# Seven block products for twelve chunks of a down projection, with weight sums formed in DRAM and the residual added there

## The chip, the cores and the metric

The kernel runs on one core of a Trainium2 chip. The time is that of one launch on the device, in microseconds (us); of several runs the median is given. A traced execution also gives its span, from the first to the last recorded instruction. The engines are TensorE (PE, matmuls; PEld its weight loads), VectorE (DVE), ScalarE (ACT), GpSimd (POOL) and SyncE (SP). SP and POOL issue the DMA transfers that this case is about. PSUM holds the sums of matmuls, SBUF the tiles.

## The reference

One layer of a decoder runs on 512 prompt tokens and 8 x 4 sample tokens, in fp32, with shared weights. A convolution mixer and a sparse attention lie beside each other ahead of a feed-forward part with 22 chunks of 128 hidden columns. What matters here is its end:

```python
x = x + g1 * ((ga * y_a + gb * y_b) @ w['w_out'])
h2 = rmsnorm(x, w['norm2']) * (1 + sc2) + sh2
x = x + g2 * ((jax.nn.silu(h2 @ w['w_gate']) * (h2 @ w['w_up'])) @ w['w_down'])
return x, nsa_state, conv_new
```

D_MODEL is 1024 and D_FF 2816. A final RMSNorm gives y. The other outputs are the new caches; one of them, new_win_sample, is the old window cache moved on by four rows, which the kernel copies from DRAM to DRAM.

## The kernel before, in words

All 544 tokens lie along the free axis, channels along the 128 partitions. A product in fp32 is made of three matmuls (`mm3`, L248): high half by high half, high by low, low by high. ACT writes the high half of an operand (a copy into the reduced type), DVE subtracts it to get the low half. Weights come from DRAM as slabs of up to 1 MB (`slab`, L232), issued by SP into three buffers, and are split after they land. The split weights have two buffers of each kind (`wh`, `wl`, `Wh`, `Wl`).

`seven` (L281) makes two output chunks of 128 columns from one slab with seven block products in place of eight. The slab is four blocks a11, a12, a21, a22. Sums of them are needed: y2 = a21 + a22, y1 = y2 + a11, z1 = a11 + a21, z2 = y1 + a12. The tokens are halved too (272 columns each), and of the right-hand side there are the blocks B11, B21, B22 and the sums T1 to T4, formed once in `combine`. A pair is the generator `wpair` (L329): products A (`wA`), B (`wB`) and C (`wC`), 12 matmuls each, then WY by T2 and T1, WZ by T3; W3 by T4 and WZ by B22 are kept in `late` and issued inside the next pair. So a pair is 84 matmuls of 272 columns. Its splits are W0 (a11, a12), WY, WZ and W3 (a22).

The feed-forward loop runs c2 = 1 to 10 (chunks 2 c2 and 2 c2 + 1; chunks 0 and 1 are made earlier). A round is a gate pair, whose outputs go through Silu into `G`, and an up pair, whose outputs are collected in `U` and multiplied into `G`, then split into `f_hilo` (`up_out`, L1717). The down projection has three phases, `PHASES = ((0, 8), (8, 8), (16, 6))`. The first two are plain (`down_part`, L1735), after rounds 3 and 7: for each of 8 output blocks m and each half of the tokens, 8 chunks by three matmuls into `dn`, then `residual` (L1550) on DVE adds the scaled result to `x1`, which stays in SBUF. The last phase is mixed with the final norm.

For c2 = 1 three of the sums are begun by DMA: SP copies a21 from DRAM into SBUF and POOL adds another block to it with an accumulating transfer (L312, L314). The copies of the window cache (`win_shift`) are issued by SP in the rounds c2 = 2 to 9.

The order in which each engine gets its instructions is fixed when the program is built, by a scheduler that goes by the program text and the dependencies. An engine then works through its own list in order: an instruction that waits holds up all behind it.

Of the kernel before, what the change touches and what calls it, by code (L numbers as in the profile page):

```python
# [1941 lines left out]
```

## Time and profile before

| | us |
|---|---|
| runs before | 1228.72, 1228.92, 1230.36 |
| median | 1228.92 |
| profiled execution | 1229.26 |
| its span | 1227.5 |
| feed-forward, first matmul of c2 = 1 to the last phase | 865.46 to 1173.83 |
| last phase and end | 1173.83 to 1227.5 |

How to read the rows: a row of single instructions has its start, its duration, engine, line of the program, operation, the tile written and read, the shape, and in brackets how long the engine stood idle before it and whom it waited for. Matmuls are pipelined, so that the durations of neighbours overlap. A row of a group has count, total busy time and mean duration in ns, then idle time ahead of it and who ended that. A row of windows has the busy time of each engine in a stretch. In DMA rows the last number is the median time from issue to landing.

### The profile page before, as it was taken

The numbers are of one execution on the slowest core, as the hardware profiler recorded it, in microseconds if no ns is written. First come the engines' busy times: TensorE is split into PE (matmuls) and PEld (weight loads), VectorE is DVE, ScalarE is ACT, GpSimd is POOL, SyncE is SP. The second block draws the span as 40 slices with busy tenths as digits, with TensorE's granted clock in tenths as the row PEclk, the third lists the DMA queues.
The fourth block names the chain that finished last, engine by engine and source line by source line (L and its number), as shares of the span: only waits on it lengthen the run. The fifth ranks groups of instructions, "written<-read, shape, count | busy, mean of one in ns | idle before, by whom it ended". The sixth has DMA issues, their size and how long they took to land.

```text
span 1227.5 us, 25476 instructions
## 1 busy us (share of the span) xinstructions
PE 1209.9 (99%) x10230; PEld 1117.1 (91%) x10230; DVE 844.1 (69%) x1868; ACT 631.4 (51%) x1214; POOL 54.8 (4%) x105
## 2 busy tenths in 40 slices
PE   8999999999999999999999999999999999999997
PEld 6998999999999988887777778999999999999996
DVE  4467646897776376676767766758975678666866
ACT  5456545665445333376666675427653255424542
POOL 1000220000000111110000000001000000000000
PEclk9999999999999999999999999999999999999999
DMA  8954234664344997975563325424533423333212
GB/s 282 407 199 155 88 123 149 215 200 164 141 136 145 355 355 277 305 235 163 174 166 121 125 83 213 133 101 138 140 121 121 154 103 137 104 109 132 87 53 73
DMA packets 58920, 205.14 MB, mean 167 GB/s; under 512 B 7208, under 2 KB 13224, under 8 KB 43578
## 3 DMA queue, kind: packets, MB, share of 16 engines
q1 hardware_dynamic: 56898, 199.57, 47.2%
q0 software_dynamic: 1472, 3.56, 1.3%
q8 instruction: 80, 1.31, 0.4%
q10 hardware_dynamic: 432, 0.39, 0.1%
q14 instruction: 38, 0.31, 0.1%
HBM read 181.60 MB, written 29.11 MB: 172 GB/s over the span
## 4 chain that ended last, share of the span: by engine, by line
PE 56%; DVE 1%; ACT 0%; issue 0%; DVEq 0%; ACTq 0%
PE lin L250 5%; PE lin L249 5%; PE lin L251 5%; PE wA L249 4%; PE dn L249 4%; PE dn L251 4%; PE dn L250 3%; PE acc L1440 3%; PE wA L250 3%; PE wA L251 3%; PE ptp L1446 3%; PE wC L251 2%; PE wC L250 2%; PE wC L249 2%; PE modp L401 1%; PE sp L1412 1%
## 5 line engine op out<-in xcount | busy, mean ns | idle before, releaser
L244 ACT ACTIVATE wh<-raw 128x1024 fp32r<-128x1024 f32 x58 | 61.3, 1057 | 99.9 <-PE dn L250 36.8
L249 PE MATMUL lin<-h_h,wh 128*128 128x288 f32 (+1 forms) x352 | 103.8, 295 | 0.0
L250 PE MATMUL lin<-h_l,wh 128*128 128x288 f32 (+1 forms) x352 | 101.6, 289 | 0.0
L251 PE MATMUL lin<-h_h,wl 128*128 128x288 f32 (+1 forms) x352 | 101.2, 288 | 0.0
L245 DVE TENSOR_TENSOR wl<-raw,wh 128x1024 fp32r<-128x1024 f32 x58 | 70.9, 1223 | 26.5 <-ACT wh L244 25.7
L249 PE MATMUL dn<-f_hilo,wh 128*128 128x288 f32 (+1 forms) x304 | 88.0, 291 | 0.1
L251 PE MATMUL dn<-f_hilo,wl 128*128 128x288 f32 (+1 forms) x304 | 87.6, 289 | 0.0
L250 PE MATMUL dn<-f_hilo,wh 128*128 128x288 f32 (+1 forms) x304 | 87.2, 287 | 0.0
L298 ACT ACTIVATE work<-wA 128x272 f32<-128x272 f32 x117 | 46.2, 395 | 66.0 <-PE wA L251 65.0
L1419 ACT ACTIVATE P<-P,nms 128x384 f32<-128x384 f32 (+3 forms) x120 | 65.0, 544 | 20.4 <-DVE nms L1418 19.8
L1418 DVE CUSTOM_DVE_ANT_0 P<-sp,ta 128x384 f32<-128x384 f32 (+3 forms) x120 | 52.4, 470 | 31.5 <-PE sp L1406 24.1
L249 PEld LDWEIGHTS lin<-h_h,wh 128*128 128x128 f32 x352 | 66.8, 190 | 7.7 <-issue 6.2
L650 PE MATMUL phi<-xh,wph 128*128 128x256 f32 x256 | 72.0, 289 | 1.3 <-ACT xh L632 0.7
L650 PE MATMUL phi<-xl,wph 128*128 128x256 f32 x256 | 70.5, 284 | 1.4 <-DVE xl L633 1.4
L383 DVE TENSOR_TENSOR Wl<-ws,Wh 128x1024 fp32r<-128x1024 f32 x39 | 47.8, 1225 | 33.8 <-ACT Wh L382 33.6
L650 PE MATMUL phi<-xh,wpl 128*128 128x256 f32 x256 | 70.2, 283 | 0.0
L250 PEld LDWEIGHTS lin<-h_l,wh 128*128 128x128 f32 x352 | 66.3, 188 | 0.1
L251 PEld LDWEIGHTS lin<-h_h,wl 128*128 128x128 f32 x352 | 66.1, 188 | 0.1
L382 ACT ACTIVATE wh<-raw 128x1024 fp32r<-128x1024 f32 (+2 forms) x43 | 44.4, 1033 | 32.6 <-PE wC L250 13.9
L382 ACT ACTIVATE wh<-ws 128x1024 fp32r<-128x1024 f32 x39 | 41.4, 1062 | 38.3 <-PE wB L250 25.0
L382 ACT ACTIVATE Wh<-ws 128x1024 fp32r<-128x1024 f32 x39 | 41.3, 1059 | 36.4 <-PE wC L250 29.2
L383 DVE TENSOR_TENSOR wl<-ws,wh 128x1024 fp32r<-128x1024 f32 x39 | 47.8, 1225 | 16.1 <-ACT wh L382 15.9
(516 smaller groups left out, 4244.8 us busy)
## 6 DMA issues: line engine op xcount, KB each, us to landing
raw<-in_wt SPq DMA_DIRECT2D x97, 1024.0 KB, 5.3
sraw<-in_cache_sel SPq DMA_DIRECT2D x64, 256.0 KB, 4.7
gt<-in_cache_cmp SPq DMA_DIRECT2D x56, 256.0 KB, 5.5
wraw<-in_cache_winT SPq DMA_DIRECT2D x8, 1024.0 KB, 8.2
out_new_win_sample<-in_cache_win SPq DMA_DIRECT2D x8, 512.0 KB, 5.7
out_new_win_sample<-in_cache_win SPq DMA_DIRECT2D x8, 504.0 KB
raw<-in_wt SPq DMA_DIRECT2D x4, 768.0 KB, 4.2
xT<-in_xT SPq DMA_DIRECT2D x1, 2176.0 KB, 13.5
```

Of the source, the lines that this page charges most:

```text
L244: act.activation(oh, view, AF.Copy)
L245: dve.tensor_sub(ol, view, oh.bitcast(F32))
L249: pe.matmul(p, lhsT=wh[:, k, :], rhs=xh, start=start, stop=False, **kw)
L250: pe.matmul(p, lhsT=wh[:, k, :], rhs=xl, start=False, stop=False, **kw)
L251: pe.matmul(p, lhsT=wl[:, k, :], rhs=xh, start=False, stop=stop, **kw)
L298: o_.snap_ops.append(act.activation(t, p, AF.Copy))
L382: act.activation(hi, src, AF.Copy)
L383: return dve.tensor_sub(lo, src, hi.bitcast(F32))
L650: pe.matmul(po[:, s * 256:s * 256 + 256], lhsT=w, rhs=m, start=(n_ == 0), stop=(n_ == len(ops) - 1))
L1418: p_ops.append(dve.tensor_tensor_reduce(out=t[:, 0:n], in0=sps[br], in1=t_dist[:, 512 - n:512], scale=-hs, scalar=3e38, op0=ALU.add, op1=A ...
L1419: e_ops.append(act.activation(t[:, 0:n], t[:, 0:n], AF.Exp, scale=-1.0, bias=nms[:, c:c + 1], accum_out=sums[:, c:c + 1]))
L1440: pe.matmul(acc[br * 64:br * 64 + 64, :], lhsT=vtok[br][:, j, g * 64:(g + 1) * 64], rhs=pts_[br], start=(j == 0), stop=False)
```

## The change

The phases of the down projection become (0, 4), (4, 6), (10, 6), (16, 6). The first, four chunks, stays plain but moves into round c2 = 2 (`down_plain`); the second and third, six chunks each, are made by `seven` with three chunks on each side of a block (`down_seven`, in rounds 5 and 8): four pairs of 7 x 3 x 3 matmuls each. The last phase is as before. For the seven products the results of the up pairs of rounds 2 to 7 are also needed in sums, which `up_seven` forms on DVE and splits.

The sums y2 and z1 of 28 slabs (20 gate and up slabs, 8 of the down projection) are formed in DRAM long before (`presum`): SP copies a21 twice into a DRAM tile, and one call later POOL adds a22 and a11 to it. The calls lie in the input projection (9), the attention (14) and the output projections. A pair then loads its two sums by one SP transfer of 512 or 384 KB into one of two buffers `ws`, and DVE forms y1 and z2 alone. The order of the blocks inside a slab is changed for that.

The residual x1 is written to DRAM (`x1_dr`, eight SP transfers) when it is formed. Down results are scaled by ACT into staging tiles (`gated`; slices of U and of the G that is not in use) and added in DRAM by 24 accumulating POOL transfers of 272 KB (`add_x1`). Eight SP transfers bring x1 back before the last phase. Its place in SBUF meanwhile holds operands of the new products (`f_x`). Eight of the sixteen window copies move ahead into the output projections.

```diff
-PHASES = ((0, 8), (8, 8), (16, 6))
+PHASES = ((0, 4), (4, 6), (10, 6), (16, 6))
...
+            r6 = np.arange(c0 * 128, (c0 + n) * 128).reshape(n, 128)
+            if ph in (1, 2):
+                quarters(("dn", ph, k2), "w_down", [k2 * 256 + m * 128 + np.arange(128) for m in range(2)], np.concatenate([r6[0::2], r6[1::2]]))
+            else:
+                add(("dn", ph, k2), "w_down", r6, k2 * 256, 256)
...
-        def wslab(*key, summed=0):
+            n_ = len(X[0]) if isinstance(X[0], list) else 4
+            xk = lambda t, k: t[k] if isinstance(t, list) else t[:, k, :]
+            k0 *= n_
+            for k in range(n_):
+                mm3(p, w[0][:, k0:k0 + n_], w[1][:, k0:k0 + n_], xk(X[0], k), xk(X[1], k), k, first and k == 0, k == n_ - 1, skip_group_check=not first)
+
+        def wslab(*key):
             raw = slab(*key)
-            y, z = (wsp.tile([128, 8, 128], F32, tag="ws", bufs=3, name=nm("ws")) for _ in range(2))
-            if summed:
-                src = lambda i: a["wt"][SLAB_AT[key], :, 512 * i:512 * i + 512]
-                for t, i in ((y[:, 4:8], 3), (z[:, 0:4], 0))[0:summed]:
-                    t = t.rearrange("p k f -> p (k f)")
-                    sync.dma_start(t, src(2))
-                    with tc.issue_after(dma_behind.ins):
-                        pool.dma_start(t, src(i), accum_op=ALU.add)
-            return raw.rearrange("p k f -> p (k f)").rearrange("p (n k f) -> p n k f", n=4, k=4), y, z, summed
+            n_ = len(SLABS[key][1]) // 4
+            if key in pre:
+                t = wsp.tile([128, 16, 128], F32, tag="ws", bufs=2, name=nm("ws"))
+                sync.dma_start(t[:, n_:3 * n_].rearrange("p k f -> p (k f)"), pre[key][:, 0:256 * n_])
+                y, z = t[:, 0:2 * n_], t[:, 2 * n_:4 * n_]
+            else:
+                y, z = (wsp.tile([128, 8, 128], F32, tag="ws", bufs=3, name=nm("ws"))[:, 0:2 * n_] for _ in range(2))
+            q = raw.rearrange("p k f -> p (k f)").rearrange("p (n k f) -> p n k f", n=4, k=n_)
+            return q, y, z, key in pre
...
+    x1_dr = [dr.tile([128, NT], F32, name=f"x1_dr{c}") for c in range(8)]
+    pre, pre_keys, copied = {}, [(n, c2) for c2 in range(1, FC // 2) for n in ("fg", "fu")], []
+    for c2 in (8, 5):
+        pre_keys[2 * c2 - 1:2 * c2 - 1] = [("dn", 1 + (c2 == 8), m2) for m2 in range(4)]
+
+    def presum(n=1):
+
+        done = copied[:]
+        del copied[:]
+        for _ in range(min(n, len(pre_keys))):
+            key = pre_keys.pop(0)
+            w_ = len(SLABS[key][1]) // 4 * 128
+            t = pre[key] = dr.tile([128, 1024], F32, name=nm("pre"))
+            src = a["wt"][SLAB_AT[key], :, 0:4 * w_].rearrange("p (n f) -> p n f", n=4)
+            dst = t[:, 0:2 * w_].rearrange("p (n f) -> p n f", n=2)
+            with tc.issue_after(last_slab[0].ins):
+                sync.dma_start(dst, src[:, 1:2].broadcast_to([128, 2, w_]))
+            copied.append((dst, src[:, 0:4:2]))
+        for dst, src in done:
+            pool.dma_start(dst, src, accum_op=ALU.add)
...
+        if hf:
+            sync.dma_start(x1_dr[k], x1[:, k, :])
...
+    f_x = x1_slot("f_x", F32R, WH)[:, 0:14]
+    g2n = modT[:, 0:8, :]
+    act.activation(g2n, g2m, AF.Copy, scale=-1.0)
...
+    def up_seven(G, c2):
+        if c2 % 3 == 2:
+            tt = [f_x[:, 4 * i:4 * i + 4] for i in range(2)]
+            bb = [f_x[:, 8 + i] for i in range(6)]
+        else:
+            tiles = [f6_tile(4 * (c2 % 3 == 0) + i, [128, 4, WH], F32R, "fs") for i in range(4)]
+            tt = tiles[0:2]
+            bb = [tiles[2 + i // 4][:, i % 4] for i in range(6)]
+        ops = fops.setdefault((c2 - 2) // 3, {n: ([], []) for n in ("B11", "B21", "B22", "T1", "T2", "T3", "T4")})
+        for n, i in (("B11", 0), ("B21", 2), ("B22", 4)):
+            for x in range(2):
+                ops[n][x].append(bb[i + x])
+        for n, t, i in (("T1", 0, 0), ("T3", 0, 1), ("T2", 1, 0), ("T4", 1, 1)):
+            for x in range(2):
+                ops[n][x].append(tt[t][:, 2 * x + i])
+        Uf = flat(U)
+
+        def out(m, q, p, s_):
+            if s_ is None:
+                dve.scalar_tensor_tensor(G[:, 1, Q[0]], p, -1.0, G[:, 1, Q[0]], ALU.mult, ALU.mult)
+                to_hilo(G[:, 1, Q[0]], bb[2], bb[3])
+                return
+            dve.tensor_add(U[:, m, Q[q]], p, s_)
+            if m == 1:
+                dve.scalar_tensor_tensor(G[:, 1, Q[1]], U[:, 1, Q[1]], -1.0, G[:, 1, Q[1]], ALU.mult, ALU.mult)
+                to_hilo(G[:, 1, Q[1]], bb[4], bb[5])
+            elif q == 1:
+                dve.tensor_mul(G[:, 0, :], U[:, 0, :], G[:, 0, :])
+                t0, t1, t3 = Uf[:, 0:WH], Uf[:, 2 * WH:3 * WH], Uf[:, 3 * WH:4 * WH]
+                dve.tensor_sub(t0, G[:, 0, Q[0]], G[:, 0, Q[1]])
+                dve.tensor_sub(Uf[:, WH:2 * WH], G[:, 1, Q[1]], G[:, 0, Q[1]])
+                to_hilo(G[:, 0, Q[0]], bb[0], bb[1])
+                pair = lambda i: Uf[:, 2 * i * WH:2 * i * WH + 2 * WH].rearrange("p (k n) -> p k n", k=2)
+                dve.scalar_tensor_tensor(t1, t0, -1.0, G[:, 1, Q[1]], ALU.mult, ALU.subtract)
+                dve.scalar_tensor_tensor(t3, G[:, 1, Q[0]], -1.0, t1, ALU.mult, ALU.subtract)
+                to_hilo(pair(0), tt[0][:, 0:2], tt[0][:, 2:4])
+                to_hilo(pair(1), tt[1][:, 0:2], tt[1][:, 2:4])
+        return out
+
+    def gated(t, c, src, m, g):
+
+        w_ = c.stop - c.start
+        s0 = TS if c.start == 0 else 0
+        act.activation(t[:, c.start + s0:c.stop], src[:, s0:w_], AF.Copy, scale=g[:, m, 0:1])
+        if s0:
+            gbc = g[:, m, 1:9].rearrange("p (b x) -> p b x", x=1).broadcast_to([128, 8, 4])
+            dve.tensor_mul(t[:, 0:TS].rearrange("p (b t) -> p b t", t=4), src[:, 0:TS].rearrange("p (b t) -> p b t", t=4), gbc)
+
+    def add_x1(m, t):
+        pool.dma_start(x1_dr[m], t, accum_op=ALU.add)
+
+    def down_plain():
+
+        nk = PHASES[0][1]
+        stg = [t[:, m, :] for t in (U, Gs[1]) for m in range(2)]
         for m in range(KC):
             if m % 2 == 0:
-                sl_ = slab("dn", ph, m // 2)
+                sl_ = slab("dn", 0, m // 2)
             w = split(sl_[:, :, (m % 2) * 128:(m % 2) * 128 + 128], nk=nk)
+            t = stg[m % 4]
             for hf in range(2):
                 p = lin_ps(nm("dn"))[:, 0:HW[hf]]
                 for k in range(nk):
-                    c = PHASES[ph][0] + k
-                    mm3(p, w[0], w[1], fh[c][:, hcols(hf)], fl[c][:, hcols(hf)], k, k == 0, k == nk - 1)
-                residual(x1, m, hf, p, g2m, f6)
+                    mm3(p, w[0], w[1], fh[k][:, hcols(hf)], fl[k][:, hcols(hf)], k, k == 0, k == nk - 1)
+                gated(t, hcols(hf), p, m, g2m)
+            add_x1(m, t)
+
+    def dn_out(m2, ts):
+        def out(m, q, p, s_):
+            t, g, c = ts[m], (g2m, g2n)[m], Q[q]
+            if s_ is not None:
+                dve.tensor_add(t[:, c], p, s_)
+                p = t[:, c]
+            gated(t, c, p, 2 * m2 + m, g)
+            if m != q:
+                add_x1(2 * m2 + m, t)
+        return out
+
+    def down_seven(ph):
+        o_ = SimpleNamespace(**fops[ph - 1])
+        u0, u1, v0, v1 = (t[:, m, :] for t in (U, Gs[ph - 1]) for m in range(2))
+        for m2, ts in enumerate(((u0, u1), (v0, v1), (u1, u0), (v1, v0))):
+            yield wslab("dn", ph, m2), dn_out(m2, ts), o_
...
     for c2 in range(1, FC // 2):
         G = Gs[c2 % 2]
-        gate = wpair(wslab("fg", c2, summed=2 * (c2 == 1)), gate_out(G))
-        win_shift(c2 - 2, 0)
+        gate = wpair(wslab("fg", c2), gate_out(G), tie=last_mod[0] if c2 == 1 else None)
+        if c2 in range(2, 10):
+            win_shift(4 + (c2 - 2) // 2, c2 % 2)
         next(gate)
         if c2 > 1:
             next(late[0], None)
             next(gate)
-        ffn_tiles(2 * c2), ffn_tiles(2 * c2 + 1)
-        up = wpair(wslab("fu", c2, summed=int(c2 == 1)), up_out(G, 2 * c2))
-        win_shift(c2 - 2, 1)
+        if c2 == 2:
+            finish_pair()
+            down_plain()
+        if c2 in (5, 8):
+            for slabs, out, o_ in down_seven(1 + (c2 == 8)):
+                dn = wpair(slabs, out, o_=o_)
+                next(dn)
+                next(late[0], None)
+                next(dn)
+        if not 2 <= c2 <= 7:
+            ffn_tiles(2 * c2), ffn_tiles(2 * c2 + 1)
+        up = wpair(wslab("fu", c2), up_seven(G, c2) if 2 <= c2 <= 7 else up_out(G, 2 * c2), tie=last_mod[0] if c2 == 1 else None)
         next(up)
         if c2 == 1:
             next(gate)
         next(late[0], None)
         next(up)
-        for ph in range(2):
-            if 2 * c2 + 2 == PHASES[ph + 1][0]:
-                finish_pair()
-                down_part(ph)
     finish_pair()
+    x1 = x1_slot("x1b", F32)
+    for k in range(KC):
+        with tc.issue_after(last_slab[0].ins):
+            sync.dma_start(x1[:, k, :], x1_dr[k])
```

The first place is DVE's list where an up pair ends and other work begins. In the kernel before, the last product of the up pair of round 4 (`wC_12668`) is followed by the up pair of round 5.

```order
L1728 TENSOR_TENSOR work<-wC_12668,work 128x272 [waits PE_49]
L383 TENSOR_TENSOR wl_12845<-raw_12839,wh_12844 128x1024 [waits Activation_49]
L1720 TENSOR_TENSOR work<-work 128x544 [waits DVE_49]
L1710 TENSOR_TENSOR work<-wC_12793,work 128x272 [waits Activation_49]
L348 TENSOR_TENSOR ws_12965<-raw_12962 128x512
L383 TENSOR_TENSOR f_hilo_12587<-work,f_hilo_12587 128x544 [waits Activation_49]
L350 TENSOR_TENSOR ws_12965<-ws_12964,raw_12962 128x512
L1728 TENSOR_TENSOR work<-wB_12862,work 128x272 [waits PE_49,Activation_49]
L383 TENSOR_TENSOR wl_12898<-ws_12842,wh_12897 128x1024 [waits Activation_49]
L383 TENSOR_TENSOR Wl_12902<-raw_12839,Wh_12901 128x512 [waits PE_49,Activation_49]
```

In the changed kernel the last product of the up pair of round 4 is `wC_12574`, L1814, and the first pair of the down projection (`raw_12749`, `ws_12751`) follows the gate pair of round 5.

```order
L1814 TENSOR_TENSOR work<-wC_12574,work 128x272 [waits PE_49]
L359 TENSOR_TENSOR ws_12856<-ws_12856,raw_12854 128x384 [waits DMAHW2_49,DMAHW1_49]
L1819 TENSOR_TENSOR work<-work 128x544 [waits DVE_49]
L397 TENSOR_TENSOR wl_12754<-raw_12749,wh_12753 128x768 [waits Activation_49]
L1821 TENSOR_TENSOR work<-work 128x272 [waits DVE_49]
L1822 TENSOR_TENSOR work<-work 128x272
L397 TENSOR_TENSOR fs_12500<-work,fs_12500 128x272 [waits Activation_49]
L1825 SCALAR_TENSOR_TENSOR work<-work 128x272 [waits DVE_49]
L1767 TENSOR_TENSOR work<-wC_12697,work 128x272
L1826 SCALAR_TENSOR_TENSOR work<-work 128x272 [waits DVE_49]
L397 TENSOR_TENSOR fs_12498<-work,fs_12498 128x544 [waits Activation_49]
L397 TENSOR_TENSOR wl_12801<-ws_12751,wh_12800 128x768 [waits PE_49,Activation_49]
```

Behind the last add of the up pair stood one product and one split of its result; now there are two subtractions, two combined products and three splits between the weight splits.

The second place is DVE's list between the second and the third of these pairs. L1863 adds a snapshot to a product into a staging tile (`work`), L1838 scales the 32 sample tokens.

```order
L397 TENSOR_TENSOR wl_12905<-ws_12856,wh_12904 128x768 [waits Activation_49]
L397 TENSOR_TENSOR Wl_12909<-raw_12854,Wh_12908 128x384 [waits PE_49,Activation_49]
L1838 TENSOR_TENSOR work<-wA_12757,modT 128x32 [waits Activation_49]
L397 TENSOR_TENSOR Wl_13002<-ws_12958,Wh_13001 128x768 [waits PE_49,Activation_49]
L1863 TENSOR_TENSOR work<-wC_12818,work 128x272 [waits PE_49]
L397 TENSOR_TENSOR wl_12961<-raw_12956,wh_12960 128x768 [waits Activation_49]
L359 TENSOR_TENSOR ws_13060<-ws_13060,raw_13058 128x384 [waits DMAHW6_49,DMAHW5_49,DVE_49]
L1863 TENSOR_TENSOR work<-wC_12922,work 128x272 [waits Activation_49]
L364 TENSOR_TENSOR ws_13060<-ws_13060,raw_13058 128x384 [waits DVE_49]
L1863 TENSOR_TENSOR work<-wB_12975,work 128x272 [waits DMASW3_49,PE_49,Activation_49]
L1838 TENSOR_TENSOR work<-work,modT 128x32 [waits DVE_49]
L397 TENSOR_TENSOR wl_13007<-ws_12958,wh_13006 128x768 [waits Activation_49]
```

The row on `wB_12975`, the first result of the third pair, waits for DMASW3, a POOL transfer: the add into DRAM that last read its staging tile. The split of WZ of the third pair (`wl_13007`) stands behind it. There was no such wait in this part of DVE's list.

The third place is SP's list at the start of the feed-forward part, before:

```order
L235 DMA raw_11256<-in_wt 128x2048 [waits DMAHW1_49,DMAHW6_49,DVE_49,Activation_49]
L312 DMA ws_11258<-in_wt 128x512 [waits PE_49,Pool_49]
L312 DMA ws_11259<-in_wt 128x512 [waits DMAHW3_49,DMASW2_49,DMASW1_49]
L312 DMA ws_11300<-in_wt 128x512 [waits DMAHW4_49]
L235 DMA raw_11298<-in_wt 128x2048 [waits DMAHW7_49,DVE_49]
L235 DMA raw_11482<-in_wt 128x2048 [waits DMAHW0_49,DVE_49]
```

and now, from the last of the eight writes of x1 (`x_dr`) on:

```order
L1626 DMA x_dr_112<-x_9824 128x544 [waits DMAHW5_49,DVE_49]
L240 DMA raw_11404<-in_wt 128x2048 [waits DMAHW6_49,DVE_49]
L240 DMA raw_11585<-in_wt 128x2048 [waits DMAHW7_49,DVE_49]
L1570 DMA out_new_win_sample<-in_cache_win 64x2048 [waits DMAHW0_49]
L318 DMA ws_11368<-pre_2924 128x1024 [waits DMASW2_49,DMASW3_49,DMASW0_49,DMAHW1_49,PE_49,Pool_49]
L318 DMA ws_11406<-pre_3216 128x1024 [waits DMAHW2_49,DMASW1_49,DVE_49]
L318 DMA ws_11587<-pre_3487 128x1024 [waits DMAHW3_49,DMAHW1_49,DVE_49]
L240 DMA raw_11735<-in_wt 128x1024 [waits DMAHW4_49,DVE_49]
L318 DMA ws_12017<-pre_3744 128x1024 [waits DMAHW5_49,DMAHW2_49,DVE_49]
```

The loads of the sums for the first pairs (`ws_11368` and two more) have moved behind the slabs of two pairs, a window copy and the writes of x1.

More of the change, by code (lines that the diff above doesn't have):

```diff
@@ L111, in _slabs, with quarters @@
     add(("gate",), "w_in", r, C_GATE, 128)
-    def quarters(key, src, cols):
-        d[key] = (src, np.concatenate([r, r]), np.concatenate([np.tile(c, (8, 1)) for c in cols]))
+    def quarters(key, src, cols, rows=r):
+        n = len(rows)
+        d[key] = (src, np.concatenate([rows[n // 2:], rows[:n // 2], rows]), np.concatenate([np.tile(c, (n, 1)) for c in cols[::-1]]))
     for v in range(2):
@@ L279, in blocks, with seven @@
         return tuple(x[n][:, kq[k], Q[q]] for n in range(2))
-    def seven(o_, ww, wlp, wsp, behind=None, dma_behind=None):
+    def seven(o_, ww, wlp, wsp):
         wi, ns, late = [0], [0], [iter(())]
@@ L324, in prepare @@
+        def prepare(slabs):
+            raw, y, z, summed = slabs
+            n_ = raw.shape[2]
+            y1, y2, z1, z2 = y[:, 0:n_], y[:, n_:2 * n_], z[:, 0:n_], z[:, n_:2 * n_]
+            a22, a21, a11, a12 = (raw[:, i] for i in range(4))
+            W0 = wsplit(raw[:, 2:4].rearrange("p n k f -> p (n k) f"))
+            if not summed:
+                dve.tensor_add(y2, a21, a22)
+            dve.tensor_add(y1, y2, a11)
             WY = wsplit(y)
-            dve.tensor_add(z[:, 0:4], a11, a21)
@@ L326, in prepare, with wpair @@
-            dve.tensor_add(z[:, 4:8], y[:, 0:4], a12)
+            if not summed:
+                dve.tensor_add(z1, a11, a21)
+            dve.tensor_add(z2, y1, a12)
             return W0, WY
-        def wpair(slabs, out, ready=None):
+        def wpair(slabs, out, ready=None, o_=o_, tie=None):
             raw, y, z, summed = slabs
-            a11, a12, a21, a22 = (raw[:, i] for i in range(4))
-            W0 = wsplit(raw[:, 0:2].rearrange("p n k f -> p (n k) f")) if ready is None else ready[0]
+            n_ = raw.shape[2]
+            y1, y2, z1, z2 = y[:, 0:n_], y[:, n_:2 * n_], z[:, 0:n_], z[:, n_:2 * n_]
+            a22, a21, a11, a12 = (raw[:, i] for i in range(4))
+            W0 = wsplit(raw[:, 2:4].rearrange("p n k f -> p (n k) f")) if ready is None else ready[0]
@@ L337, in wpair @@
             pB = lin_ps(nm("wB"))[:, 0:WH]
-            product(pB, W0, 4, o_.B21, True)
+            product(pB, W0, 1, o_.B21, True)
             out(0, 0, pB, s1)
@@ L358, in wpair @@
             pC = lin_ps(nm("wC"))[:, 0:WH]
-            product(pC, WY, 4, o_.T1, True)
+            product(pC, WY, 1, o_.T1, True)
             next(late[0], None)
@@ L370, in rest @@
                 yield
-                product(pC, WZ, 4, o_.B22, False)
+                product(pC, WZ, 1, o_.B22, False)
                 out(0, 1, pC, s2)
@@ L1751, in finish_pair @@
             pass
-    def win_shift(b, h_):
-        if b not in range(DEC_B):
-            return
-        rows = lambda z: z.rearrange("(n t) w -> n (t w)", t=4)
-        src, dst = rows(a["cache_win"][b, 4:512, :]), rows(o["new_win_sample"][b])
-        with tc.issue_after(last_slab[0].ins):
-            sync.dma_start(dst[h_::2], src[h_::2])
     for c2 in range(1, FC // 2):
         G = Gs[c2 % 2]
-        gate = wpair(wslab("fg", c2, summed=2 * (c2 == 1)), gate_out(G))
-        win_shift(c2 - 2, 0)
+        gate = wpair(wslab("fg", c2), gate_out(G), tie=last_mod[0] if c2 == 1 else None)
+        if c2 in range(2, 10):
+            win_shift(4 + (c2 - 2) // 2, c2 % 2)
         next(gate)
```

49 lines of the change are left out of this document (27 added, 22 removed).

## Prediction

> **What bounds the kernel now.** I read the page first, then a table of the feed-forward stage by stretches, then the order of single matmuls in it.
>
> ```profile
> span 1227.5 us, 25476 instructions
> PE 1209.9 (99%) x10230; PEld 1117.1 (91%) x10230; DVE 844.1 (69%) x1868; ACT 631.4 (51%) x1214; POOL 54.8 (4%) x105
> ```
> The profiled execution took 1229.26 us, 1.76 more than its span and 0.34 more than the median, 1228.92. TensorE is busy 99% of it, so only fewer TensorE cycles, or a new wait, can move the end. The next rows cut the feed-forward at the changes of work: seven-product pairs, the plain down projection of 8 chunks with pairs after it, the second of these, pairs, last phase. Columns: length, then busy time (instructions) of PE, PEld, DVE, ACT and POOL, granted clock, DMA share, GB/s.
>
> ```profile
> 865.46:926.70 61.24, 61.24 (x482) 60.42 (x481) 48.79 (x73) 35.74 (x57) 0.00 (x0) 1.00 0.38 132
> 926.70:1026.00 99.30, 99.27 (x785) 98.34 (x784) 68.10 (x116) 38.81 (x58) 0.00 (x0) 1.00 0.34 123
> 1026.00:1112.50 86.50, 86.50 (x684) 85.59 (x683) 55.38 (x95) 32.17 (x46) 0.00 (x0) 1.00 0.37 132
> 1112.50:1173.80 61.30, 61.26 (x482) 60.43 (x481) 45.81 (x68) 35.01 (x55) 0.00 (x0) 1.00 0.25 86
> 1173.80:1227.50 53.70, 45.31 (x352) 43.49 (x350) 35.87 (x100) 16.81 (x35) 1.57 (x2) 0.95 0.16 57
> ```
> TensorE is full in the first four, DVE is at 80% (48.79 of 61.24) where pairs run and DMA at a third: TensorE sets the time, DVE is next. What a matmul costs has to be read from starts, because the durations overlap:
>
> ```profile
> 882.32 0.28 PE L249 MATMUL wA<-T_hi,wh 128*128 128x272 f32 x1
> ...
> 894.38 0.29 PE L249 MATMUL wA<-h_hi,wh 128*128 128x272 f32 x1
> ...
> 894.76 0.28 PE L250 MATMUL wB<-h_lo,wh 128*128 128x272 f32 x1
> 895.03 0.39 PE L249 MATMUL wA<-h_hi,Wh 128*128 128x272 f32 x1
> ...
> 905.17 0.29 PE L249 MATMUL wA<-h_hi,wh 128*128 128x272 f32 x1
> ```
> From 882.32 to 894.38 there are 96 matmuls in 12.06 us: 0.1256 us each, not the 0.28 that a row states. A pair of 84 should take 10.55; from 894.38 to 905.17 it took 10.79. The missing 0.24 lies near 894.76 to 895.03, where TensorE waits for the next pair's first weight split. The plain down projection does not lose that:
>
> ```profile
> 942.23 1.06 ACT L244 ACTIVATE wh<-raw 128x1024 fp32r<-128x1024 f32 x1 [4.90 <-PE dn L250]
> ...
> 966.27 1.06 ACT L244 ACTIVATE wh<-raw 128x1024 fp32r<-128x1024 f32 x1 [4.90 <-PE dn L250]
> ```
> Four chunks of 48 matmuls in 24.04 us are 0.1252 each.
>
> **The change part by part.** *Matmuls.* The plain phases had 2 x 384 = 768 matmuls before the last phase. Now there are 192 for four chunks, and 8 pairs of 7 x 3 x 3 = 63, which is 504: 696, so 72 fewer. 72 x 0.1256 = **9.0 us saved**. The sheet of busy times would say 72 x 0.289 = 20.8; the starts exclude it.
>
> [...]
>
> *Losses inside the eight new pairs.* In a pair of 84 the split begins when the buffer is freed by the last product of the pair before, and runs ACT then DVE:
>
> ```profile
> 892.95 1.06 ACT L382 ACTIVATE wh<-raw 128x1024 fp32r<-128x1024 f32 x1 [0.38 <-PE wC L250]
> 894.10 1.22 DVE L383 TENSOR_TENSOR wl<-raw,wh 128x1024 fp32r<-128x1024 f32 x1
> ```
> From 892.88, where that product ends, to 895.32 is 2.44 us. In a new pair the split has 768 columns, and these rows price everything that follows on DVE and ACT (count, total and mean ns):
>
> ```profile
> L383 DVE TENSOR_TENSOR wl<-raw,wh 128x768 fp32r<-128x768 f32 x1 | 1.0, 959 | 0.2 <-ACT wh L382 0.2
> L382 ACT ACTIVATE wh<-raw 128x768 fp32r<-128x768 f32 x1 | 0.8, 848 | 0.7 <-PE wC L250 0.7
> L383 DVE TENSOR_TENSOR wl<-ws,wh 128x1024 fp32r<-128x1024 f32 x20 | 24.5, 1225 | 9.3 <-ACT wh L382 9.3
> L348 DVE TENSOR_TENSOR ws<-raw 128x512 f32<-128x512 f32 x19 | 13.0, 684 | 0.0
> L1728 DVE TENSOR_TENSOR work<-wC,work 128x272 f32<-128x272 f32 x18 | 7.8, 435 | 0.0
> L1720 DVE TENSOR_TENSOR work<-work 128x544 f32<-128x544 f32 x9 | 6.5, 722 | 0.1
> L1722 DVE SCALAR_TENSOR_TENSOR work<-work 128x272 f32<-128x272 f32 x9 | 3.9, 438 | 0.1
> L383 DVE TENSOR_TENSOR f_hilo<-work,f_hilo 128x272 fp32r<-128x272 f32 x18 | 7.9, 438 | 2.0 <-ACT f_hilo L382 2.0
> L383 DVE TENSOR_TENSOR f_hilo<-work,f_hilo 128x544 fp32r<-128x544 f32 x9 | 6.5, 722 | 1.1 <-ACT f_hilo L382 1.1
> L298 ACT ACTIVATE work<-wA 128x272 f32<-128x272 f32 x59 | 23.3, 394 | 17.3 <-PE wA L251 16.5
> L1557 DVE TENSOR_TENSOR rs_t<-dn,modT 128x32 f32<-128x32 f32 x16 | 2.9, 181 | 0.0
> ```
> 0.85 + 0.96 and the same 0.16 of hand-over make 1.97, against a cover of one product of 9 matmuls and the 7 that need only high halves: 16 x 0.1256 = 2.01. So the loss should almost vanish. Bounds: 0 and 8 x 0.24 = 1.9; I take 0.4. DVE in such a pair: three splits 2.88, one of 384 columns and two sums of 384 (0.56 each, between the 272 and 512 rows) 1.68, three adds 1.31, two 32-column products 0.36: 6.2 of 63 x 0.1256 = 7.9 us. It fits.
>
> *Sums taken off DVE, operands put on it.* Each of 20 gate and up pairs loses two sums of 0.684: 2.74 per chunk pair (gate and up). In six chunk pairs DVE gains two subtractions and two combined products (4 x 0.44), one split of 272 (0.44) and one of 544 (0.72): 2.92. Summing durations, DVE goes from 20.3 to 20.5 of a 21.6 us round (2 x 10.79), though neighbouring rows overlap a little, so the window showed 80%. This is a draw: 0 most likely, 2 us if two of the six rounds are late by 1. The 0.24 of a gate or up pair is no DVE queue but the chain above, so relieving DVE in the other rounds gives nothing back; if it did, the bound is 20 x 0.24 = 4.8 of gain. I take a loss of 0.3.
>
> *The two entries into the new pairs* (c2 = 5 and 8) are the worst place. After the last product of the preceding up pair, DVE must finish: an add 0.44, one sum of 384 columns 0.56, the product 0.72, the weight split 0.96, two subtractions 0.88, a split 0.44, a combined product 0.44, an add 0.44, another combined product 0.44, a split of 544 0.72, a weight split 0.96, a split of 544 0.72: 7.7 us in a line, with ACT's halves in between. TensorE has about 60 matmuls before the last of them is needed, 7.5 us. With two or three hand-overs of some 0.2 that is 0.7 to 0.9 late. Bounds: 0 (the scheduler's order covers it) and 2.5 each (the hand-overs all exposed); I take 0.9 each, 1.8. Before, one add, one product, one 544 split and the weight split stood there, 2.8 us in all.
>
> *The residual* leaves DVE: ACT scales PSUM into a staging tile (0.39 as its copies) and POOL adds the tile into DRAM. A staging tile is written again 54 matmuls after the earlier pair's last product, in the third and fourth pair of a phase, 60 at the following up pair, 84 in the plain phase. 54 x 0.1256 = 6.8 us, less 0.6 for ACT and the hand-over: 6.2 us for a landing. No such add is in the trace; the nearest rows are POOL transfers (KB each, median us to landing):
>
> ```profile
> ws<-in_wt POOLq DMA_DIRECT2D x3, 256.0 KB, 9.5
> gb_dr<-gb POOLq DMA_DIRECT2D x2, 272.0 KB, 4.5
> tf<-tf POOLq DMA_DIRECT2D x1, 544.0 KB, 4.8
> tf<-h_full POOLq DMA_DIRECT2D x1, 544.0 KB, 7.1
> ```
> The second is the same size and direction without the add; the last two add twice as much inside SBUF; the first adds out of DRAM while two 1 MB slabs load. I take 6, nearest to the middle two, and that is covered. DVE is what would wait, and behind it the third pair's splits, which TensorE needs 36 matmuls (4.5 us) later: a landing up to about 8 costs nothing. Lower bound 0, upper bound below (rival 3); I take 0.4.
>
> *Transfers.* 28 copies on SP and 28 adds on POOL form the sums between the projections and the output stage, where TensorE was full even with DMA near its limit:
>
> ```profile
> 260.00:280.00 20.00, 20.00 (x158) 19.76 (x158) 17.42 (x27) 11.75 (x19) 0.00 (x0) 1.00 0.61 206
> 400.00:420.00 20.00, 20.00 (x170) 19.50 (x169) 8.81 (x29) 8.43 (x14) 3.77 (x9) 1.00 0.96 347
> 620.00:640.00 20.00, 20.00 (x157) 13.81 (x155) 11.40 (x45) 11.78 (x32) 0.00 (x0) 1.00 0.70 190
> ```
> Nothing reads a sum until hundreds of us later, so I cost them at 0; without that cover it would be a late slab, up to 1 us at a place. At the start of the feed-forward SP now has eight writes of x1 and the loads of the first sums behind the slabs:
>
> ```profile
> 845.17 3.42 SPq L235 DMA_DIRECT2D raw<-in_wt  x2
> 848.92 0.60 SPq L1760 DMA_DIRECT2D out_new_win_sample<-in_cache_win  x1
> ...
> L345 DVE TENSOR_TENSOR ws<-ws,raw x2: 689/690/692, 859.2 to 863.5; 128x512 f32<-128x512 f32 x2
> raw<-in_wt SPq DMA_DIRECT2D x97, 1024.0 KB, 5.3
> ```
> The sums are issued near 849.5; one landing of 5.3 behind the slabs brings the first to about 856, 3 us before DVE reads it: 0, or 1 to 2 if the queue drains slowly. The reload of x1 before the last phase has a full pair to land: 0.
>
> Sum: -9.0 + 0.4 + 0.3 + 1.8 + 0.4 = **-6.1**, so 1223.2 profiled, **1222.8** against the median.
>
> **The rivals.** *1, the full count:* entries and staging are covered, -9.0 + 0.4: 1220.3. For it: the first four stretches show PE busy for their whole length. Against: the 7.7 us line at the entries. *2, DVE becomes the bound:* entries 2.5 each, six rounds late by 0.4 each, pairs 0.24 each: 5 + 2.4 + 1.9 = 9.3, all of the saving, 1229.2; half as bad, 1226. For it: 20.5 of 21.6 us. Against: the window's 80%. *3, the adds land late (the other side):* if a landing takes 9.5, DVE stands 3.3 us in the third pair, has 1.7 to spare per pair, and TensorE pays about 2.5 a phase; at the 12 us that a busy stretch could make of it, 5 to 6 a phase. Two phases: 5 and 11 us, so 1228 and 1234. It eats the saving from a landing of about 10, and makes the kernel slower by more than 0.2% from about 11. For it: the 9.5 row is a POOL add. Against: the two adds inside SBUF, and DMA at a third.
>
> [...]
>
> **How the numbers follow.** About 0.2% (2.5 us) is what a measurement here can tell. Forecast 0.53 (own range 1220 to 1226), rival 1 0.20, rival 2 0.15, rival 3 0.12. Faster: the first two, and a third of the second rival, 0.77; same: the rest of rival 2 and a little of 3, 0.13; slower 0.10. Ends: 1219 is the full count with a little given back by DVE's relief; 1229 is rival 2 in full or the adds at 9.5.
>
> **What would show it.** The feed-forward (308.4 us from 865.46 to the last phase at 1173.83) should shrink by about 6. Pairs of 63 should be 7.9 apart; the rounds with c2 = 2 to 7 still 21.6; TensorE idle 0.5 to 1 us at the two entries, on VectorE's splits. x_dr adds should land in 5 to 7 us, with no VectorE row released by them. The forecast is wrong if VectorE waits on POOL's adds in each third pair, if a round grows past 22, or if stages before 860 move by over 1 us.

## The result, and the profile after

The change made the kernel slower: 1246.12 us median (1244.05 to 1246.92, four runs) against 1229.14 for the kernel before; the ratio is 1.0134, with a 95% interval of 1.0116 to 1.0151. The forecast was 1222.8, the range ended at 1229.0, and slower had a chance of 0.10.

The page of the changed kernel, its first lines and the row of the queue that POOL feeds (packets, MB, share of 16 engines):

```profile
span 1242.3 us, 25810 instructions
PE 1209.3 (97%) x10158; PEld 1113.3 (90%) x10158; DVE 845.0 (68%) x1891; ACT 673.5 (54%) x1323; POOL 100.1 (8%) x154
...
q0 software_dynamic: 12112, 23.09, 11.4%
```

TensorE has the 72 instructions fewer, but as much busy time as before (1209.9) and 15 us more of span. Three windows place it: up to the first pair of c2 = 1, from there to the last phase, and the rest. Before:

```profile
0.00:865.46 865.46, 856.30 (x7457) 768.78 (x7458) 590.10 (x1420) 472.87 (x965) 53.18 (x103) 1.00 0.57 191
865.46:1173.83 308.37, 308.30 (x2426) 304.81 (x2425) 218.12 (x350) 141.73 (x214) 0.00 (x0) 1.00 0.34 120
```

After:

```profile
0.00:865.88 865.88, 854.44 (x7456) 768.47 (x7457) 586.55 (x1416) 471.41 (x965) 77.88 (x128) 1.00 0.72 228
865.88:1188.77 322.89, 309.59 (x2355) 301.42 (x2354) 222.66 (x376) 185.31 (x323) 20.66 (x24) 0.98 0.55 170
1188.77:1242.30 53.53, 45.25 (x352) 43.42 (x350) 35.79 (x100) 16.75 (x35) 1.58 (x2) 0.96 0.16 57
```

Everything is in the middle one: 322.89 against 308.37. TensorE stands still for 13.3 us of it (322.89 less 309.59), and the mean granted clock is 0.98. DMA is busy 0.55 there, 0.34 before.

The largest waits lie in the two phases of new pairs. Single instructions of the first of them, POOL's adds:

```profile
1004.04 0.86 POOL L1841 DMA_DIRECT2D x_dr<-work  x1 [75.10 <-DVE work L1838]
...
1015.96 0.86 POOL L1841 DMA_DIRECT2D x_dr<-work  x1 [7.76 <-DVE work L1838]
```

VectorE:

```profile
1008.08 0.55 DVE L364 TENSOR_TENSOR ws<-ws,raw 128x384 f32<-128x384 f32 x1
1013.56 0.44 DVE L1863 TENSOR_TENSOR work<-wB,work 128x272 f32<-128x272 f32 x1 [4.92 <-PE wC L255]
...
1024.65 0.44 DVE L1863 TENSOR_TENSOR work<-wB,work 128x272 f32<-128x272 f32 x1 [4.46 <-DMA x_dr<-work]
```

ScalarE:

```profile
1014.03 0.49 ACT L1835 ACTIVATE work<-work,modT 128x240 f32<-128x240 f32 x1 [3.69 <-DVE work L1863]
...
1015.19 0.38 ACT L303 ACTIVATE work<-wA 128x272 f32<-128x272 f32 x1
```

TensorE:

```profile
1009.24 0.28 PE L256 MATMUL wB<-fs,wl 128*128 128x272 f32 x1
...
1013.36 0.29 PE L256 MATMUL wC<-fs,wl 128*128 128x272 f32 x1
1015.63 0.39 PE L254 MATMUL wA<-f_x,wh 128*128 128x272 f32 x1 [1.97 <-ACT work L303]
```

This is the third pair. Its first result, `wB`, was complete at 1009.5, yet VectorE took it at 1013.56: the staging tile still fed the add issued at 1004.04, 9.5 us earlier. (The row names PE; the second one, at 1024.65, names the add, issued at 1015.96, 8.7 us earlier.) ScalarE's copy of that result waits for VectorE, and behind the copy stands the snapshot of `wA` (L303). TensorE may not add to `wA` before it, so it stands until 1015.63. VectorE's other waits on the adds, and TensorE's on the snapshot, in the table of waits (total, times, longest):

```profile
DVE work L1863 <- DMA x_dr<-work: 12.6, 3, 5.2
DVE work L1767 <- DMA x_dr<-work: 5.1, 1, 5.1
PE wA L254 <- ACT work L303: 9.1, 7, 2.7
```

The single wait of L1767 belongs to the gate pair behind the first of these phases. Its first result goes into the half of `G` that served as a staging tile, and the add that reads this tile was issued 10.7 us earlier:

```profile
1036.64 0.86 POOL L1841 DMA_DIRECT2D x_dr<-work  x1 [5.71 <-DVE work L1838]
...
1047.32 0.44 DVE L1767 TENSOR_TENSOR work<-wB,work 128x272 f32<-128x272 f32 x1 [5.09 <-DMA x_dr<-work]
```

After three of TensorE's pauses behind such waits (2.27, 2.16 and 3.00 us from one matmul's start to the next) the matmuls start 0.226 us apart for some 2.5 to 3.5 us, then 0.126 again. The windows behind the first and third (columns as above, with the granted clock third from the end):

```profile
1015.60:1019.10 3.50, 3.47 (x17) 3.46 (x18) 2.79 (x5) 2.24 (x4) 1.46 (x2) 0.60 0.82 307
1019.10:1024.00 4.90, 4.90 (x39) 4.90 (x38) 1.09 (x3) 1.77 (x3) 0.26 (x1) 0.94 1.00 280
...
1132.60:1135.60 3.00, 2.96 (x13) 2.96 (x14) 2.11 (x4) 2.30 (x3) 0.86 (x1) 0.50 0.79 273
1136.00:1145.00 9.00, 9.00 (x74) 9.00 (x73) 5.61 (x10) 5.37 (x8) 1.71 (x2) 1.00 0.75 198
```

17 matmuls in 3.5 us and 13 in 3.0 is the clock at about half (granted 0.60 and 0.50 in these windows), and TensorE counts as busy in it (3.47 and 2.96). About 41 matmuls, each some 0.10 us longer, are 4 us of busy time, a part of why it did not fall with 72 matmuls fewer.

Three smaller places remain. At the start:

```profile
873.01 0.40 PE L254 MATMUL wA<-T_hi,wh 128*128 128x272 f32 x1 [0.92 <-ACT wh L396]
874.88 0.40 PE L256 MATMUL wA<-T_hi,wl 128*128 128x272 f32 x1 [1.10 <-DVE wl L397]
```

In the plain phase of c2 = 2, where VectorE's next row is the sum for a pair to come, whose slab is late, and the split that TensorE needs now stands behind it:

```profile
922.10 0.69 DVE L359 TENSOR_TENSOR ws<-ws,raw 128x512 f32<-128x512 f32 x1 [3.54 <-DMA raw<-in_wt]
922.71 0.68 DVE L250 TENSOR_TENSOR wl<-raw,wh 128x512 fp32r<-128x512 f32 x1
```

And behind that phase, where VectorE waits for sums that are loaded late:

```profile
936.15 0.69 DVE L359 TENSOR_TENSOR ws<-ws,raw 128x512 f32<-128x512 f32 x1 [4.45 <-DMA ws<-pre]
```

### The profile page after: what moved, and what is told of

Its sections match the earlier page's. It is cut to its first block, busy times and chain, and to the rows that moved or that the text cites. A ratio compares the mean times of both kernels' runs of the same rounds, so it can differ in the third digit from the quotient of the medians.

```text
span 1242.3 us, 25810 instructions
## 1 busy us (share of the span) xinstructions
PE 1209.3 (97%) x10158; PEld 1113.3 (90%) x10158; DVE 845.0 (68%) x1891; ACT 673.5 (54%) x1323; POOL 100.1 (8%) x154
## 4 chain that ended last, share of the span: by engine, by line
PE 41%; issue 9%; DMA 4%; DVE 3%; ACT 2%; POOL 1%; DVEq 0%; ACTq 0%; POOLq 0%
PE lin L255 5%; PE lin L254 4%; PE lin L256 4%; PE acc L1477 3%; PE ptp L1483 3%; PE wA L254 2%; PE wA L256 2%; PE wA L255 2%; PE modp L415 1%; PE dn L256 1%; PE dn L254 1%; DMA x_dr<-work 1%; PE dn L255 1%; DMA raw<-in_wt 1%; PE sp L1449 1%
## 5 line engine op out<-in xcount | busy, mean ns | idle before, releaser
L303 ACT ACTIVATE work<-wA 128x272 f32<-128x272 f32 x141 | 55.3, 393 | 73.8 <-PE wA L256 70.9
L397 DVE TENSOR_TENSOR Wl<-ws,Wh 128x1024 fp32r<-128x1024 f32 (+1 forms) x47 | 55.4, 1179 | 40.1 <-ACT Wh L396 38.9
L250 DVE TENSOR_TENSOR wl<-raw,wh 128x1024 fp32r<-128x1024 f32 (+1 forms) x50 | 56.8, 1136 | 34.0 <-ACT wh L249 33.5
L249 ACT ACTIVATE wh<-raw 128x1024 fp32r<-128x1024 f32 (+1 forms) x50 | 49.3, 986 | 52.4 <-PE lin L255 31.4
L397 DVE TENSOR_TENSOR wl<-ws,wh 128x1024 fp32r<-128x1024 f32 (+1 forms) x47 | 55.3, 1178 | 13.8 <-ACT wh L396 13.1
L396 ACT ACTIVATE Wh<-ws 128x1024 fp32r<-128x1024 f32 (+1 forms) x47 | 48.0, 1021 | 28.6 <-PE wC L255 26.2
L396 ACT ACTIVATE wh<-ws 128x1024 fp32r<-128x1024 f32 (+1 forms) x47 | 48.1, 1024 | 27.7 <-PE wB L255 24.4
L397 DVE TENSOR_TENSOR wl<-raw,wh 128x1024 fp32r<-128x1024 f32 (+2 forms) x51 | 58.6, 1149 | 2.0 <-ACT wh L396 2.0
L558 POOL DMA_DIRECT2D pre<-in_wt x28 | 27.2, 972 | 370.7 <-DMA pre<-in_wt 370.7
L685 PEld LDWEIGHTS phi<-xh,wph 128*128 128x128 f32 x256 | 47.5, 189 | 4.0 <-ACT wph L593 1.8
```

Source lines behind the costliest of these rows:

```text
L249: act.activation(oh, view, AF.Copy)
L250: dve.tensor_sub(ol, view, oh.bitcast(F32))
L303: o_.snap_ops.append(act.activation(t, p, AF.Copy))
L396: act.activation(hi, src, AF.Copy)
L397: return dve.tensor_sub(lo, src, hi.bitcast(F32))
L685: pe.matmul(po[:, s * 256:s * 256 + 256], lhsT=w, rhs=m, start=(n_ == 0), stop=(n_ == len(ops) - 1))
```

## The experiments

The theory formed on this trace, S: the waits on the adds, through VectorE and ScalarE, and the half clock behind them cost most of the loss. Rivals: VectorE or ScalarE has too much to do in the new phases (D); the sums formed in DRAM disturb the rest (P). Each "before" below is the run of the kernel before on the same chip.

**Adds by halves.**

```diff
             gated(t, c, p, 2 * m2 + m, g)
-            if m != q:
-                add_x1(2 * m2 + m, t)
+            pool.dma_start(x1_dr[2 * m2 + m][:, c], t[:, c], accum_op=ALU.add)
...
-        for m2, ts in enumerate(((u0, u1), (v0, v1), (u1, u0), (v1, v0))):
+        for m2, ts in enumerate(((u0, u1), (v0, v1), (u0, u1), (v0, v1))):
```

> The changed kernel, but each half of a staging tile is added into DRAM as soon as it is written (16 adds of 136 KB in each of the two six-chunk phases, in place of 8 of 272 KB), and the tiles are taken in the same order each second pair; a half is then written again 126 matmuls, 15.8 us, after its add, in place of 54 matmuls, 6.8 us. Theory S (VectorE's four waits on the adds, the ScalarE copies behind them and the half clock that follows cost most of the loss): 13 to 15 us faster than the changed kernel, 1231 to 1233, no VectorE row released by x_dr. Rival D (VectorE or ScalarE has too much to do in these phases, the adds only happen to be last): less than 4 us better, 1242 to 1246. Rival P (the sums formed in DRAM disturb other stages): within 2 us of 1246.

Measured 1232.16 (before 1229.94; ratio 1.0015, 1.0005 to 1.0024): 14.0 better than the changed kernel, and VectorE has no wait on `x_dr` left. S holds for most of the loss; D falls, since VectorE's and ScalarE's work is the same. The edit does two things, smaller adds and a longer time until a tile is written again (126 matmuls in place of 54); they were not run apart.

**No sums in DRAM.**

```diff
-    for c2 in (8, 5):
+    del pre_keys[:]
+    for c2 in ():
```

> The changed kernel without the sums formed in DRAM: VectorE forms all four sums of each pair, as before the change; everything else as changed. Theory S: the waits on the adds stay; each round of gate and up gets 2.7 us more on VectorE, 23.2 us by summed durations against 21.6 of TensorE, so 2 to 10 us slower than the changed kernel, 1248 to 1256. Rival P: 1232 to 1238, because copies, adds and late loads of sums are gone.

Measured 1234.55 (before 1229.94; 1.0035, 1.0021 to 1.0049): 11.6 better, which only P had expected. The adds still make VectorE wait, but less, and no pause is over 1.5 us, and the half clock does not follow. The adds in the list of DMA issues:

```profile
x_dr<-work POOLq DMA_DIRECT2D x24, 272.0 KB, 6.5
```

and the waits on them:

```profile
DVE work L1864 <- DMA x_dr<-work: 7.3, 2, 3.9
DVE work L1768 <- DMA x_dr<-work: 4.8, 2, 4.0
```

In the changed kernel the landing was 7.5, and up to 10.6:

```profile
x_dr<-work POOLq DMA_DIRECT2D x24, 272.0 KB, 7.5
```

```profile
DMA to landing us min/median/max: 4.0/7.5/10.6
```

(the list of DMA issues, and the view of the tile for POOL alone). So the two theories meet: with the sums' transfers the adds take longer in the median. The rounds did not get longer from the extra work on VectorE: the pairs of rounds 3 and 4 start 10.53 to 10.80 apart. My 23.2 of 21.6 us was wrong as a bound, since neighbouring rows of VectorE overlap (in the changed kernel that of 922.10 lasts to 922.79, and the next starts at 922.71).

**The first sums loaded earlier**, and with adds by halves.

```diff
-            raw = slab(*key)
+            with tc.issue_after(ws_op[0].ins) if ws_op and key in (("fu", 1), ("fg", 2)) else ExitStack():
+                raw = slab(*key)
...
-                sync.dma_start(t[:, n_:3 * n_].rearrange("p k f -> p (k f)"), pre[key][:, 0:256 * n_])
+                ws_op[:] = [sync.dma_start(t[:, n_:3 * n_].rearrange("p k f -> p (k f)"), pre[key][:, 0:256 * n_])]
```

> The changed kernel with SP's loads of the sums for the gate and up pairs of c2 = 1 put ahead of the slabs of the next pairs. If the 3.2 us that TensorE loses at the start of the feed-forward (871 to 880 us) come from sums that land late or are placed late in VectorE's list for that reason, 2 to 3 us better, 1243 to 1244; if they come from the order of the other splits there, no difference, 1245 to 1247. Theory S says nothing on it.

> The adds by halves and the early loads of the first sums together. Theory S with the start: 1228 to 1231, about the time of the kernel before; rivals D and P: 1240 or more.

Measured 1251.15 and 1235.57 (before 1229.94 for both): 5.0 and 3.4 worse than without. The gate pair's load moved as meant (from 849.95 to 844.40 in the changed kernel), the up pair's did not (867.51 and 869.03). VectorE's list changed with them: the up pair's first split stands at 874.58 in place of 858.24, and the first pair took 18.4 and 17.5 us in place of 14.1 and 15.3. (The first pair is measured here and below from its first matmul to its last product in `wA`, W3 by T4: 84 matmuls in the kernel before.) This does not isolate the cause; the run without these sums, below, does.

**Both remedies.** Adds by halves and no sums in DRAM, the first two edits together.

> Both at once: adds by halves, and no sums formed in DRAM (VectorE forms them). What remains of the change is then the seven products for twelve chunks and the residual in DRAM. Theory S2 (the waits on the adds cost by themselves, and the traffic and late loads of the sums cost apart from that): the second run's 1234.6 less its seven waits of 0.5 to 1.5 us in the two phases, 1226 to 1228.5, faster than the kernel before by 1.5 to 4. Rival O (the two remedies act on one and the same wait): 1231 to 1234.

Measured 1225.52 (before 1229.39; 0.9964, 0.9951 to 0.9978): faster than the kernel before, and 20.6 better than the changed kernel. Two causes, then, and not one; they overlap, since the two remedies alone gave 14.0 and 11.6. Without the sums VectorE's waits on the adds, in the rows above, are already 12.1 in place of 17.7.

**The sums alone**, in the kernel before.

```diff
-PHASES = ((0, 4), (4, 6), (10, 6), (16, 6))
+PHASES = ((0, 8), (8, 8), (16, 6))
...
-        up = wpair(wslab("fu", c2), up_seven(G, c2) if 2 <= c2 <= 7 else up_out(G, 2 * c2), tie=last_mod[0] if c2 == 1 else None)
+        up = wpair(wslab("fu", c2), up_out(G, 2 * c2), tie=last_mod[0] if c2 == 1 else None)
...
+        for ph in range(2):
+            if 2 * c2 + 2 == PHASES[ph + 1][0]:
+                finish_pair()
+                down_part(ph)
```

(The writes of x1 to DRAM, its reload and the seven products are out.)

> The kernel before with the sums of the 20 gate and up slabs formed in DRAM and the slab order and window copies as changed; the down projection as before in plain phases, the residual in SBUF. Theory S2: no gain on TensorE, since VectorE was not the limit; the losses at the start of the feed-forward (3 us) and ahead of it (0.5 to 1.5) remain: 1232 to 1235. Rival V (the relief of VectorE, 2.7 us a round, is worth something, as the count of idle on VectorE's splits suggests): 1225 to 1229.

Measured 1232.31 (before 1229.39; 1.0023, 1.0013 to 1.0033). The middle window of this run:

```profile
865.61:1178.08 312.47, 310.29 (x2426) 306.36 (x2425) 198.20 (x316) 142.59 (x215) 0.00 (x0) 0.99 0.38 137
```

VectorE has 20 us less to do (218.12 before, 198.20 here) and the stage is 4.1 longer. All of that is the first pair: 15.20 us, 11.24 before; every later pair agrees within 0.12, all but the second within 0.04. Relief of VectorE is worth nothing here, and the sums cost the start.

**Sums on VectorE for c2 = 1 only**, with adds by halves.

```diff
-    pre, pre_keys, copied = {}, [(n, c2) for c2 in range(1, FC // 2) for n in ("fg", "fu")], []
+    pre, pre_keys, copied = {}, [(n, c2) for c2 in range(2, FC // 2) for n in ("fg", "fu")], []
```

> The adds by halves, and the sums of the slabs of c2 = 1 alone formed by VectorE in place of DRAM. If the start of the feed-forward is lost because the first sums cannot be loaded earlier: 3 us better than the adds by halves alone, 1228.5 to 1230; if not, 1231 to 1233.

Measured 1229.63 (before 1229.39; 1.0004, 0.9994 to 1.0013): 2.5 better than adds by halves alone; the first pair takes 11.58 us, not 15.30. (The sums of c2 = 1 use the two buffers `ws` here too.) So the start was lost to these sums. In the changed kernel VectorE forms the first y1 at 869.52, behind the first pair's first result, where the kernel before formed it at 859.22; TensorE's two waits at 873.01 and 874.88 are on the splits of it. The load of these sums was issued at 849.95, and such loads land after 3.4 us in the median: it was not late.

**Plain writes in place of adds.**

```diff
-        pool.dma_start(x1_dr[m], t, accum_op=ALU.add)
+        pool.dma_start(x1_jk[m], t)
```

> The changed kernel with the 24 POOL transfers as plain writes into another DRAM tile, not as adds; so the two middle phases and the first one are left out of the residual. Same queue, size, staging tiles. If it is the add itself (a read and a write back in DRAM) that makes the landing long: landing 4 to 5 us as the plain POOL writes of the kernel before, no wait at the staging tiles, 1231 to 1234. If it is the queue or the traffic beside it: landing 7 us and about 1245.

Measured 1233.21 (before 1229.39; 1.0037, 1.0024 to 1.0051): as the first alternative had it in time, but the landing lies between the two, and VectorE still waits. The list of DMA issues:

```profile
x_jk<-work POOLq DMA_DIRECT2D x24, 272.0 KB, 5.9
```

The waits on these writes:

```profile
DVE work L1864 <- DMA x_jk<-work: 6.3, 2, 3.6
DVE work L1815 <- DMA x_jk<-work: 1.7, 1, 1.7
```

The add itself is 1.6 us of the landing of 7.5. The plain write takes 5.9, where two of the same size in the kernel before took 4.5 in the median; queue and traffic are what is left for that, and they were not separated.

**Two slabs in the plain phase**, on top of both remedies, and the same with sums for all pairs but those of c2 = 1.

```diff
-                add(("dn", ph, k2), "w_down", r6, k2 * 256, 256)
+                w_ = 512 if ph == 0 else 256
+                add(("dn", ph, k2), "w_down", r6, k2 * w_, w_)
...
-            if m % 2 == 0:
-                sl_ = slab("dn", 0, m // 2)
-            w = split(sl_[:, :, (m % 2) * 128:(m % 2) * 128 + 128], nk=nk)
+            if m % 4 == 0:
+                sl_ = slab("dn", 0, m // 4)
+            w = split(sl_[:, :, (m % 4) * 128:(m % 4) * 128 + 128], nk=nk)
```

> Adds by halves, no sums in DRAM, and the plain phase in c2 = 2 reads two slabs of 1 MB in place of four of 512 KB, so that the next up and gate slabs find a free buffer earlier. If the 2.4 us still lost in that phase (40.59 us from the gate pair to the up pair against about 38.2) is VectorE waiting at the head of its list for a slab that comes late, 2 to 2.5 us better than without: 1223 to 1223.8; if the plain phase is limited otherwise, 1225 to 1226.

> The same with the sums formed in DRAM again, for all pairs but those of c2 = 1. Theory S2: the sums give nothing on TensorE and cost a little by traffic and by SP's longer list, so 1 to 4 us slower than the run without them, 1224 to 1228. Rival V (VectorE's relief shows once the waits are gone): faster than the run without them.

Measured 1223.41 (before 1228.88; 0.9955, 0.9941 to 0.9968) and 1227.71 (0.9992, 0.9983 to 1.0001). The first is the fastest version, 5.5 under the kernel before. Its middle window:

```profile
867.33:1169.52 302.19, 301.74 (x2354) 296.50 (x2353) 251.54 (x427) 186.18 (x322) 34.41 (x40) 1.00 0.50 138
```

302.19 is 6.2 less than before, and the plain phase takes 37.85 us in place of 40.59. The sums, with everything else in order, cost 4.3 us. In that trace VectorE waits for late loads of sums, 3.52 us behind the plain phase and, in the second phase of new pairs, here:

```profile
1104.47 0.56 DVE L366 TENSOR_TENSOR ws<-ws,raw 128x384 f32<-128x384 f32 x1 [2.67 <-DMA ws<-pre]
```

The pair with this wait and the one behind it take 9.70 and 8.74 us, against 8.17 and 8.21 in the fastest version.

## Why the prediction was wrong

A table of distances between the starts of pairs in the traces (the first matmul of a pair's first product, in us) gives the loss by place; the row of the first pair is measured as above. The fastest version serves as the one without waits.

| place | changed kernel | fastest version | difference |
|---|---|---|---|
| first pair | 14.11 | 11.83 | 2.3 |
| c2 = 2: gate with the plain phase | 39.15 | 37.85 | 1.3 |
| gate and up of c2 = 3 | 11.41, 11.58 | 10.52, 10.79 | 1.7 |
| first phase of new pairs and three behind | 9.23, 8.07, 10.82, 11.33, 10.13, 13.87, 11.10 | 9.20, 8.08, 8.15, 8.21, 9.96, 10.87, 10.79 | 9.3 |
| second phase, the same | 9.44, 8.09, 8.61, 12.64, 10.21, 10.78, 11.36 | 9.21, 8.07, 8.17, 8.21, 9.96, 10.85, 10.79 | 5.9 |

Together 20.5, of the 20.7 between 322.89 and 302.19. In a phase the first distance holds 69 matmuls (24 are left over from the gate pair), the next three 63, the fifth 78 and the last two 84.

- **The residual** (0.4 in the sum) is the step that failed. The two phases lost 15.2; with adds by halves they lose 1.5, so that the late adds cost some 13.6. The wait itself was named (rival 3), and its slack, 6.2, was nearly right: at the first wait 5.5 us passed from the add's issue to the result (1004.04 to 1009.5). Two things were not right. The landing was taken as 6, the median was 7.5, and the five adds that VectorE waited for had been issued 7.5 to 10.7 us before. The rows behind the 6 come from stretches with a DMA share of 0.61 and 0.72 (536 to 551 and 858 to 868 us of the kernel before). While the five adds were on the way the share was 0.80 to 0.98; the "DMA at a third" that spoke against the rival is an average over the stage. A part of that traffic the change itself adds (the loads of sums). And the price of a late landing was too small: a landing of 9.5 was to cost 2.5 a phase, and even 12 no more than 5 to 6. The step looked only at the weight split behind VectorE's wait, due 36 matmuls later. ScalarE's list was not followed. There the scaled copy waits for VectorE, and the snapshot behind it holds `wA` and with it TensorE. 4 us of the loss are the half clock after the pauses (41 matmuls, 0.10 longer each).
- **Transfers at 0** was the second failure. The sums alone cost 2.9 (the run of the sums alone), at the very place that was named, the start of the feed-forward. "1 to 2 if the queue drains slowly" looked at the landing of the first sums, which was in time; their place in VectorE's list decides, and the trace before cannot show that. In the changed kernel they also lengthen the adds, and their later loads are late themselves: the 1.7 lost at c2 = 3 stand behind the wait of 4.45 at 936.15. Adds by halves, which has the sums, loses 2.0 there, the version with both remedies nothing (10.55, 10.79).
- **The plain phase** had no loss in the sum. It lost 1.3 here, and 2.7 in the version with both remedies (40.59), with four half-size slabs: each keeps one of three buffers for 6 us of matmuls only, so the slabs of the next pairs come late, and VectorE, in order, waits for them ahead of a split that is due (3.54 us at 922.10 in the changed kernel). With two slabs it takes 37.85. The prediction carried over the 0.1252 of a phase with full slabs.
- **The two entries** (1.8) cost little. In the fastest version the gate pair ahead takes 10.78, and the first new pair's 69 matmuls 9.20, 0.53 over 0.1256 each, where the other new pairs are 0.16 to 0.30 over: about 0.3 an entry, not 0.9. Most of the 7.7 us line of VectorE is covered. The exit costs nothing (9.96 for 78 matmuls, 0.16 over).
- **Inside the new pairs** the loss was put at 0.05 each and is 0.16 to 0.30 (8.07 to 8.21 against 7.91); some 1.9 for the eight, the upper bound.
- **VectorE's load** (0.3): nothing. In the fastest version, where VectorE has the new operands and the sums as well, the pairs of rounds 3, 4, 6 and 7 start 10.52 to 10.87 apart. Rival 2 was wrong at both of its places.
- **The saving of 9.0** is right. In the fastest version the stage is 6.2 shorter; with 2.5 in the new pairs, entries included, and 0.6 in the first pair the count is 9.3.

The rows were right on TensorE; the error was in costing the waits by the engine that waits first.

## What to carry to other kernels

A staging tile that a transfer reads is a wait for whoever writes it next (17.7 us of VectorE's waits in the changed kernel): count its slack in matmuls (6.2 us here), set it against the slowest landing under the traffic of the changed kernel (10.6 here), and follow the wait through every in-order list behind it (here VectorE, then ScalarE, then a PSUM tile) to TensorE. Releasing the tile piece by piece (each half added as soon as it is written), with the tiles taken in an order that leaves more time until the next write, needed no further tile and took 14 us off. Work taken from an engine that is not the bound bought nothing here (VectorE with 20 us less to do, the stage 4.1 longer, in the run of the sums alone), and its transfers were paid for elsewhere (the first pair, 15.20 us in place of 11.24).
